# Attention with pairs of heads tied to the tiles of v, remainders on VectorE, x on one queue, and conv's output parts ahead of the next tile

## The chip, the cores and the metric

The kernel runs on one core of a Trainium2 chip. The metric is the device time of one execution in microseconds, as the median of three runs. Engines are TensorE (PE, with its weight loads as PEld), VectorE (DVE), ScalarE (ACT), GpSimd (POOL) and SyncE (SP), which here only issues DMAs. L12 is line 12 of the kernel before.

## The reference

A decoder trunk of two layers over 256 tokens of width 1024, all in float32. Each layer is a mixer followed by a PEER expert retrieval; each part has an RMS norm in front and a residual add behind.

```python
for i in range(DEPTH):                       # DEPTH = 2
    hn = rms_norm(x, norm_mix[i])
    if i % 2 == 0:                           # b, c, z = split(hn @ w_in); u = c * z
        x = x + short_conv_mixer(hn, ...)    # (b * causal_conv3(u)) @ w_out
    else:
        x = x + moba_mixer(hn, w_qkv, w_o)   # 16 heads of 64, rotary q and k, causal softmax
    x = x + peer_ffn(rms_norm(x, norm_ffn[i]), ...)
return rms_norm(x, norm_final)
```

With 256 tokens there is one block of keys, so the attention is plain causal attention: softmax(q k' / 8) v for each head, then the product with w_o.

## The kernel before

**Weight tiles.** All weights come in tiles ("items") of 128 x 1024 float32, 512 KB each, in one fixed list: 24 of the conv mixer's w_in (in the group order 1, 2, 0), 8 of its w_out, those of the first PEER, 24 of w_qkv (8 for q, 8 for k, 8 for v), 8 of w_o, those of the second PEER. A product in float32 is made of three cheaper ones: the weight is split into a rounded part hi and a remainder lo = raw - hi, the activations likewise into xh and xl, and TensorE sums hi·xh, hi·xl and lo·xh. One tile of such a product is twelve matmuls with 512 columns (L474, or L481 to L483 where two tiles are run together as a group, bank by bank; conv's w_in has 256 columns, L461).

**Splitting and loading.** `split_to` makes hi on ACT (L166) and lo on VectorE or, for the items in the set `on_pool`, on POOL (L171). raw, hi and lo have three buffers each, used in turn, so the split of tile n waits until TensorE has done with tile n-3, and the load of tile n (issued on SP's queue, L140 to L148) waits until the split of tile n-3 has read its buffer. `next_item` emits the split of the coming tiles (`prefetch`), then the matmuls of its tile, and then as many steps of side work as a budget in a queue (`add`, `run_side`) allows; `drain_side` empties that queue. `next_group` does the same for several tiles at once. The order in which the code emits is the order of each engine's instructions.

**Start.** x comes in four loads, on SP's and ACT's queues in turn, the norm's gain first on ACT's. TensorE runs 14 dummy matmuls (`warm`, L291), spreads the gain over the partitions (L269), runs 8 more, and then turns the normed x (L365), whose parts ACT and VectorE copy (L370, L375).

**Conv mixer.** After the third group of w_in, VectorE multiplies the gate into the result, four parts of it (L596), ACT casts each part to xh (L597), and VectorE takes the remainder xl (L591). Then w_out's eight tiles run. The first prefetch of w_out is emitted with the last tile of w_in, that is ahead of these parts.

**Attention.** While k's tiles run, q is rotated (`rope`, VectorE, L210, in four pieces by half of the tokens and of the heads), turned on TensorE (L654) and copied by ACT (L660). While v's tiles run, the side queue does the same with k (L654, L663), then the scores of the pairs of heads (L670 to L673, two banks for a pair), the row maxima on VectorE (`soft`, L677 to L681) and the exponentials on ACT (L684, L686): two pairs behind a tile. After v's last tile, v is copied out of PSUM, two parts on ACT (L729) and two on VectorE (L727), and the reciprocals are taken (L731). Then, for each pair of heads, `ptr` turns the weights on TensorE (L736, L738) into two of the four banks `hi4`, ACT copies one bank (L740) and VectorE the other (L741), and two pairs later `pv` multiplies them with v (L749 to L751). At the end the result is turned (L763), split (L766, L767), and w_o's tiles follow.

Of the kernel before, what the change touches and what calls it, by code (L numbers as in the profile page):

```python
# [22 lines left out]
D = 1024  # L23
# [9 lines left out]
WARM = 14  # L33
# [4 lines left out]
def trunk_kernel(ctx: ExitStack, tc, x, norm_mix, norm_ffn, conv_w_in, conv_w, conv_w_out,  # L38
# [79 lines left out]
    on_pool, on_dve, halved = set(range(3)), set(), {0}  # L118
    state = {"dma": 0, "tr": 0, "split": 0, "use": 0}
# [40 lines left out]
    def split_to(n):  # L160
        while state["split"] <= min(n, NI - 1):
# [4 lines left out]
            act.activation(HI[m % 3], src, AF.Copy)  # L166
# [49 lines left out]
    def next_item(mm, budget=0.0):  # L216

        n = state["use"]
        split_to(n)
        prefetch(n)  # L220
        mm(HI[n % 3], LO[n % 3])
        state.pop("rest", lambda: None)()
        state["use"] += 1
        run_side(budget)
# [28 lines left out]
    def load_x(eng, i, h):  # L253
        c = slice(h * 512, h * 512 + 512)
        eng.dma_start(x_in[:, i * D + h * 512:i * D + h * 512 + 512], x[0, i * 128:(i + 1) * 128, c])
# [16 lines left out]
    act.dma_start(GN[0:1], norm_mix[0:1])  # L272
    for i in range(2):
        load_x(sp, i, 0)
        load_x(act, i, 1)
# [19 lines left out]
    warm(8)  # L295
# [260 lines left out]
    def conv_mixer():  # L556
# [28 lines left out]
        for b in range(8):  # L585
            next_item(mm_wstat(lo4, b), 2.4)
# [13 lines left out]
        out_lo(3)  # L600
        rows_out(hi4, lo4[1::2], True)
# [5 lines left out]
    def attn_mixer():  # L607
# [80 lines left out]

        for a in range(2):
            pool.memset(qT[64 - 64 * a:128 - 64 * a, :, a], 0.0)  # L690
        for g, banks in ((0, lo4), (1, hi4), (2, lo4)):
            n = state["use"] - 3 * (g == 0)
            on_pool.update(k for k in range(n + 6, n + 14) if k % 3)
            if g:
                next_group(qkv_first(banks), None, 4.5)
            for b in range(2 if g else 3, 8):
                next_item(mm_tok(banks, XH[:, b], XL[:, b], False, b == 7), 9.0 if g == 2 else 2.5)
# [462 lines left out]
```

## Time and profile before

| | us |
|---|---|
| median of 3 runs (1857.15 to 1862.35) | 1858.34 |
| profiled execution | 1857.25 |
| its span in the trace | 1855.5 |
| TensorE busy | 1828.7 (99%) |
| VectorE busy | 1325.8 (71%) |
| ACT busy | 866.5 (47%) |
| POOL busy | 827.6 (45%) |
| TensorE's share of the chain that ended last | 89% |

A row of a timeline gives the start, the length, the engine, the line and operation, the tiles written and read with their shapes, the count of instructions put together, and in brackets the idle time of the engine in front of it with what ended it. Since matmuls are pipelined, their lengths overlap: the distance between starts tells the pace. PEclk in the windows is the clock that TensorE was granted in the stretch, 1.00 being 2.4 GHz and 0.50 1.2 GHz.

### The profile page before, as it was taken

To read this page: it belongs to the slowest core of one execution; us is meant where nothing else is said; L and a number is where in the kernel's file an instruction comes from. 1 tells how busy PE (TensorE), PEld (TensorE's weight loads), DVE (VectorE), ACT (ScalarE), POOL (GpSimd) and SP (SyncE) were. 2 spreads that over 40 slices of the span, in tenths; PEclk is the share of its full clock that TensorE was granted. 3 is DMA by queue.
4 is the path that set the end of the run, shared out by engine and by line. 5 is a ranking of instruction groups with operands and counts; after the bars stand their busy time and mean duration, and the time that the engine had idled before them with its cause. 6 is when DMAs were issued, how large, how long until landed. Compare 5 with 4: busy or idle time off the path is not lost.

```text
span 1855.5 us, 34248 instructions
## 1 busy us (share of the span) xinstructions
PE 1828.7 (99%) x12993; PEld 1642.2 (89%) x12993; DVE 1325.8 (71%) x2093; ACT 866.5 (47%) x1050; POOL 827.6 (45%) x564
## 2 busy tenths in 40 slices
PE   9999999999999999999999999999999999999998
PEld 8979999999998888888778799999999988888886
DVE  4648888777778886555554467897777788875555
ACT  4455445444444444444454454545434444444544
POOL 1048899999920000000251378899999600000000
PEclk9999999999999999999997999999999999999999
DMA  7566656555555555666551475555555555556554
GB/s 205 162 194 186 177 160 180 169 171 165 166 164 172 178 173 181 228 193 193 162 171 47 136 205 164 179 167 170 166 170 165 157 182 171 171 179 230 193 193 136
DMA packets 204587, 321.26 MB, mean 173 GB/s; under 512 B 26221, under 2 KB 157317, under 8 KB 203910
## 3 DMA queue, kind: packets, MB, share of 16 engines
q1 hardware_dynamic: 201716, 311.80, 54.8%
q10 hardware_dynamic: 2706, 7.28, 1.1%
q8 instruction: 101, 1.65, 0.4%
q14 instruction: 64, 0.52, 0.1%
HBM read 315.83 MB, written 3.15 MB: 172 GB/s over the span
## 4 chain that ended last, share of the span: by engine, by line
PE 89%; DVE 3%; DMA 3%; ACT 2%; issue 1%; POOL 1%; SPq 0%; DVEq 0%; ACTq 0%; POOLq 0%
PE psum L474 39%; PE psum L839 12%; PE psum L843 12%; PE psum L840 12%; PE psum L1003 3%; PE psum L461 3%; PE psum L503 1%; POOL lo L171 1%; DVE big L210 1%; PE psum L867 1%; DVE tr L155 1%; DVE lo L171 1%; ACT hi L166 1%; DMA raw<-in_peer_u_dram 1%; PE psum L483 1%
## 5 line engine op out<-in xcount | busy, mean ns | idle before, releaser
L171 POOL TENSOR_TENSOR lo<-tr,hi 128x512 fp32r<-128x512 f32 x496 | 732.5, 1516 | 47.2 <-ACT hi L166 43.6
L166 ACT ACTIVATE hi<-raw 128x1024 fp32r<-128x1024 f32 x336 | 355.5, 1061 | 458.1 <-PE psum L474 373.2
L171 DVE TENSOR_TENSOR lo<-raw,hi 128x1024 fp32r<-128x1024 f32 x301 | 372.4, 1238 | 272.0 <-ACT hi L166 263.8
L839 PE MATMUL psum<-xh,hi 128*128 128x256 f32 x2032 | 505.1, 286 | 1.0 <-ACT hi L166 1.0
L840 PE MATMUL psum<-xl,hi 128*128 128x256 f32 x2032 | 498.3, 283 | 0.0
L474 PE MATMUL psum<-hi,xh 128*128 128x512 f32 x1108 | 436.6, 396 | 1.3 <-ACT xh L597 1.3
L474 PE MATMUL psum<-hi,xl 128*128 128x512 f32 x1108 | 429.5, 389 | 0.0
L155 DVE STREAM_TRANSPOSE tr<-raw 128x1024 f32<-128x1024 f32 x256 | 317.3, 1239 | 143.1 <-POOL lo L171 113.4
L839 PEld LDWEIGHTS psum<-xh,hi 128*128 128x128 f32 x2032 | 389.3, 192 | 1.6 <-ACT hi L166 1.4
L840 PEld LDWEIGHTS psum<-xl,hi 128*128 128x128 f32 x2032 | 389.9, 192 | 0.2
L171 POOL TENSOR_TENSOR lo<-raw,hi 128x1024 fp32r<-128x1024 f32 (+1 forms) x42 | 85.8, 2059 | 593.2 <-ACT hi L166 494.2
L166 ACT ACTIVATE hi<-tr 128x1024 fp32r<-128x1024 f32 x256 | 270.0, 1057 | 123.6 <-DVE tr L155 87.0
L474 PE MATMUL psum<-lo,xh 128*128 128x512 f32 x1108 | 296.2, 389 | 0.0
L843 PE MATMUL psum<-xh,lo 128*128 128x256 f32 x2032 | 288.5, 284 | 6.3 <-POOL lo L171 6.3
L843 PEld LDWEIGHTS psum<-xh,lo 128*128 128x128 f32 x2032 | 263.1, 192 | 8.8 <-POOL lo L171 8.7
L474 PEld LDWEIGHTS psum<-lo,xh 128*128 128x128 f32 x1108 | 207.9, 188 | 43.5 <-DVE lo L171 0.2
L474 PEld LDWEIGHTS psum<-hi,xh 128*128 128x128 f32 x1108 | 208.0, 188 | 42.3 <-ACT xh L597 1.5
L474 PEld LDWEIGHTS psum<-hi,xl 128*128 128x128 f32 x1108 | 208.3, 188 | 41.0
L975 ACT ACTIVATE big<-psum 128x512 f32<-128x512 f32 x126 | 75.3, 597 | 285.7 <-PE psum L843 285.7
L1102 POOL TENSOR_TENSOR big<-xbuf,big 128x256 f32<-128x256 f32 x2 | 1.4, 733 | 379.7 <-DVE rstd L341 379.7
L988 DVE TENSOR_TENSOR xbuf<-iota_t,eT 128x1536 f16<-128x1536 f16 x128 | 126.7, 990 | 15.3 <-PE psum L1003 15.0
L996 DVE TENSOR_TENSOR xbuf<-xbuf,gT 128x1024 f16<-128x1024 f16 x128 | 99.6, 778 | 1.1
(172 smaller groups left out, 1473.3 us busy)
## 6 DMA issues: line engine op xcount, KB each, us to landing
raw<-in_peer_u_dram SPq DMA_DIRECT2D x1024, 128.0 KB, 2.8
raw<-in_peer_v_dram SPq DMA_DIRECT2D x256, 512.0 KB, 3.4
raw<-in_conv_w_in_dram SPq DMA_DIRECT2D x96, 128.0 KB, 2.6
raw<-in_attn_w_qkv_dram SPq DMA_DIRECT2D x96, 128.0 KB, 2.6
raw<-in_peer_w_q_dram SPq DMA_DIRECT2D x64, 128.0 KB, 2.6
raw<-in_conv_w_out_dram SPq DMA_DIRECT2D x8, 512.0 KB, 3.6
raw<-in_attn_w_o_dram SPq DMA_DIRECT2D x8, 512.0 KB, 3.3
x_dram<-xbuf ACTq DMA_DIRECT2D x2, 1024.0 KB, 4.8
```

What stands on the lines that cost most here:

```text
L155: dve.transpose(TR[m % 3].rearrange("p b (g i) -> p g b i", g=4), RAW[m % 3].rearrange("p (g m) -> p g m", m=256))
L166: act.activation(HI[m % 3], src, AF.Copy)
L171: eng.tensor_sub(LO[m % 3][:, c], src[:, c], HI[m % 3][:, c])
L461: pe.matmul(banks[c // 2][:, (c % 2) * 256:(c % 2) * 256 + 256], w[:, c * 128:c * 128 + 128], xx[:, b], start=(b == 0 and p == 0 and c % 2 ...
L474: pe.matmul(banks[j], x[:, j // 2 * 128:j // 2 * 128 + 128], w[:, j % 2 * 512:j % 2 * 512 + 512], start=(first and p == 0), stop=(last and ...
L839: pe.matmul(o, hi[:, s], XH[:, b], start=(b == 0), stop=False)
L840: pe.matmul(o, hi[:, s], XL[:, b], start=False, stop=False)
L843: pe.matmul(o, lo[:, s], XH[:, b], start=False, stop=(b == 7))
L975: act.activation(A[:, k - 1:k + 1].rearrange("p k t -> p (k t)"), bk, AF.Gelu)
L988: dve.tensor_tensor(HOT[s % 2].rearrange("p b (r k) t -> p b r k t", r=3), iota_t[:, None, None].to_broadcast([128, TOK // 2, 3, 64, 2]), ...
L996: dve.tensor_tensor(OHG[s % 2], one_hot[:, None].to_broadcast([128, 2, TOK // 2, 64, 2]), gT2[:, s, :, :, None, :].to_broadcast([128, 2, T ...
L1003: pe.matmul(o, pairs[:, t // 2, :, t % 2], OHG[s % 2][:, a, t // 2, :, t % 2], start=(a == 0), stop=(a == 1))
```

## The change

It has five parts.

1. Start: the 22 dummy matmuls run in one piece ahead of the spread of the gain. All four loads of x and the gain are issued on SP's queue, the gain third; ACT issues none of them.
2. Conv: the last tile of w_in's third group is emitted without its prefetch; that comes after the four parts of the result and their remainders.
3. Attention's splits: the remainders of w_qkv's and w_o's tiles that were on POOL are made on VectorE, all but one (tile 18 of the 32), and the hi casts of the tiles 21 to 25 too (L168 of the changed kernel).
4. k and the heads: the side queue is replaced by `run_heads(b)`, which ties each step to a tile of v. A pair's two banks are now every second one, by the pair's parity (`hi4[p % 2::2]`). Three of k's four ropes are emitted ahead of v's tiles, the fourth behind the turning of k's first half. Smaller budgets move each of the two turnings of q behind one tile more.
5. v and the weights: ACT copies v's first token half and VectorE its second. `ptr(0)` runs ahead of v's last tile.

```diff
-WARM = 14
+WARM = 22
...
-            act.activation(HI[m % 3], src, AF.Copy)
+            if m in hi_dve:
+                dve.tensor_copy(HI[m % 3], src)
+            else:
+                act.activation(HI[m % 3], src, AF.Copy)
...
-    def next_item(mm, budget=0.0):
+    def next_item(mm, budget=0.0, ahead=True):
...
-        prefetch(n)
+        if ahead:
+            prefetch(n)
...
-    act.dma_start(GN[0:1], norm_mix[0:1])
     for i in range(2):
-        load_x(sp, i, 0)
-        load_x(act, i, 1)
+        for h in range(2):
+            load_x(i, h)
+        if i == 0:
+            sp.dma_start(GN[0:1], norm_mix[0:1])
...
     warm(WARM)
     spread_gain(hi4[2:4])
-    warm(8)
...
         for b in range(8):
-            next_item(mm_wstat(lo4, b), 2.4)
+            next_item(mm_wstat(lo4, b), 2.4, b < 7)
         drain_side()
...
         out_lo(3)
+        prefetch(n - 1)
         rows_out(hi4, lo4[1::2], True)
...
+        def turn_k(h):
+            for c in range(2):
+                turn(kr, 4 * h + 2 * c, hi4[h + 2 * c])
+                put_k(4 * h + 2 * c, hi4[h + 2 * c])
+
+        def heads(*ps):
+            for f in (scores, soft):
+                for p in ps:
+                    f(p, hi4[p % 2::2])
...
+        def run_heads(b):
+
+            if b == 0:
+                turn_k(0)
+                rope(kr, hi4, 1, 1)
+                drain_side()
+            elif b == 2:
+                heads(0)
+                turn_k(1)
+            elif b < 6:
+                heads(2 * b - 5, 2 * b - 4)
+            elif b == 6:
+                heads(7)
+                ptr(0)
...
-            on_pool.update(k for k in range(n + 6, n + 14) if k % 3)
+            if g == 0:
+                on_pool.add(n + 18)
+                hi_dve.update(range(n + 21, n + 26))
             if g:
-                next_group(qkv_first(banks), None, 4.5)
+                next_group(qkv_first(banks), None, 2.5 * (g == 1))
+            if g == 2:
+                run_heads(0)
             for b in range(2 if g else 3, 8):
-                next_item(mm_tok(banks, XH[:, b], XL[:, b], False, b == 7), 9.0 if g == 2 else 2.5)
+                next_item(mm_tok(banks, XH[:, b], XL[:, b], False, b == 7), 2.5 * (g < 2))
+                if g == 2:
+                    run_heads(b)
...
-                for h in range(2):
-                    for i in range(2):
-                        rope(kr, hi4, i, h)
+                for i, h in ((0, 0), (1, 0), (0, 1)):
+                    rope(kr, hi4, i, h)
                 drain_side()
-                for h in range(2):
-                    pause(h)
-                    for c in range(2):
-                        add(0.1, turn, kr, 4 * h + 2 * c, hi4[h + 2 * c])
-                        add(0.1, put_k, 4 * h + 2 * c, hi4[h + 2 * c])
-                for p in range(0, 8, 2):
-                    pause()
-                    for f in (scores, soft):
-                        for a in range(2):
-                            add(0.5, f, p + a, hi4[2 * a:2 * a + 2])
-        for i in range(2):
-            for h in range(2):
-                v = va[:, i, h * 512:h * 512 + 512]
-                if h:
-                    dve.tensor_copy(v, lo4[2 * i + h])
-                else:
-                    act.activation(v, lo4[2 * i + h], AF.Copy)
+        for h in range(2):
+            act.activation(va[:, 0, h * 512:h * 512 + 512], lo4[h], AF.Copy)
+            dve.tensor_copy(va[:, 1, h * 512:h * 512 + 512], lo4[2 + h])
...
-            b0, b1 = hi4[2 * (p % 2):2 * (p % 2) + 2]
+            b0, b1 = hi4[p % 2::2]
...
         for p in range(10):
-            if p < 8:
+            if 0 < p < 8:
                 ptr(p)
```

In the lists below hi_72 to hi_74, lo_75 to lo_77 and raw_66 to raw_68 are the three buffers of each kind; line numbers of the changed kernel are a few higher (its L170 and L175 are L166 and L171, its L712 and L713 are L740 and L741).

VectorE around the end of v's tiles, before: the last minimum of a pair, a remainder, the copies of v, the reciprocals, and the copies of turned weights.

```order
L681 TENSOR_TENSOR big<-big 128x2
L171 TENSOR_TENSOR lo_75<-raw_66,hi_72 128x1024
L727 COPY big<-psum 128x512 x2
L731 RECIPROCAL big<-big 128x32
L741 COPY big<-psum 128x2x256 x6
```

The same place of the changed kernel:

```order
L687 TENSOR_TENSOR big<-big 128x2
L713 COPY big<-psum 128x2x256
L168 CAST hi_72<-raw_66 128x1024
L175 TENSOR_TENSOR lo_75<-raw_66,hi_72 128x1024
L761 COPY big<-psum 128x512 x2
L763 RECIPROCAL big<-big 128x32
L713 COPY big<-psum 128x2x256 x5
```

The first copy of turned weights has moved ahead of the split of a w_o tile, whose cast is now here too.

ACT from the turning of k to the first exponentials, before: two copies of turned k (L663) with a hi cast between and behind them.

```order
L663 ACTIVATE big<-psum 128x512 x2
L166 ACTIVATE hi_73<-raw_67 128x1024
L663 ACTIVATE big<-psum 128x512 x2
L166 ACTIVATE hi_74<-raw_68 128x1024
L684 ACTIVATE big<-psum,big 128x128
L686 ACTIVATE big<-psum,big 128x256
```

The same place of the changed kernel, where L669 copies k and L690 and L692 are the exponentials:

```order
L669 ACTIVATE big<-psum 128x512 x2
L170 ACTIVATE hi_73<-raw_67 128x1024
L690 ACTIVATE big<-psum,big 128x128
L692 ACTIVATE big<-psum,big 128x256
L690 ACTIVATE big<-psum,big 128x128
L692 ACTIVATE big<-psum,big 128x256
L669 ACTIVATE big<-psum 128x512 x2
```

The second half of k is copied behind the exponentials of the first pair of heads.

ACT at the end of w_in's third group in the conv mixer, before: casts of weights, and the four casts of the result (L597).

```order
L166 ACTIVATE hi_74<-raw_68 128x1024
L166 ACTIVATE hi_72<-raw_66 128x1024
L166 ACTIVATE hi_73<-raw_67 128x1024
L597 ACTIVATE xh<-psum 128x512 x4
```

The same place of the changed kernel (L602 casts the result):

```order
L170 ACTIVATE hi_74<-raw_68 128x1024
L170 ACTIVATE hi_72<-raw_66 128x1024
L602 ACTIVATE xh<-psum 128x512 x4
L170 ACTIVATE hi_73<-raw_67 128x1024
```

The hi cast of w_out's second tile has moved behind the four casts.

## Rows read from the trace of the kernel before

**Rows 1.** Windows: stretch, length, busy PE PEld DVE ACT POOL, PEclk, DMA, GB/s

```profile
929.50:932.90 3.40, 1.73 (x7) 0.84 (x6) 0.78 (x1) 1.49 (x2) 2.95 (x2) 1.00 0.53 154
971.30:977.40 6.10, 6.10 (x35) 4.97 (x33) 3.27 (x7) 4.01 (x17) 0.00 (x0) 1.00 0.42 127
992.40:999.20 6.80, 3.01 (x18) 1.85 (x17) 4.10 (x8) 4.50 (x15) 0.00 (x0) 0.98 0.45 142
999.00:1003.00 4.00, 4.00 (x22) 4.00 (x20) 0.92 (x2) 0.38 (x1) 0.00 (x0) 0.50 0.10 40
...
1029.70:1034.00 4.30, 4.30 (x20) 3.56 (x19) 0.95 (x2) 3.54 (x5) 1.49 (x1) 1.00 0.02 4
```

**Rows 2.** Timeline of PE, end of attention and the tiles of w_o

```profile
992.44 0.27 PE L736 MATMUL psum<-ident,big 128*128 128x128 f32 x1
...
998.69 0.47 PE L738 MATMUL psum<-ident,big 128*128 128x128 f32 x2 [1.69 <-DVE big L741]
...
1029.11 1.43 PE L474 MATMUL psum<-hi,xh 128*128 128x512 f32 x4
...
1045.58 0.50 PE L483 MATMUL psum<-lo,xh 128*128 128x512 f32 x1 [0.52 <-DVE lo L171]
```

**Rows 3.** Timelines of ACT and DVE, the same stretch

```profile
994.29 1.09 ACT L166 ACTIVATE hi<-raw 128x1024 fp32r<-128x1024 f32 x1
995.23 1.11 ACT L729 ACTIVATE big<-psum 128x512 f32<-128x512 f32 x2
...
995.41 1.23 DVE L171 TENSOR_TENSOR lo<-raw,hi 128x1024 fp32r<-128x1024 f32 x1 [2.67 <-ACT hi L166]
...
998.01 1.22 DVE L741 COPY big<-psum 128x512 f32<-128x512 f32 x2
```

**Rows 4.** Page, costliest groups: POOL's remainders of plain weight tiles

```profile
L171 POOL TENSOR_TENSOR lo<-raw,hi 128x1024 fp32r<-128x1024 f32 (+1 forms) x42 | 85.8, 2059 | 593.2 <-ACT hi L166 494.2
```

**Rows 5.** Chain that ended last: start, length, a run of 68 tiles

```profile
710.40 185.06 PE psum L474 x816
```

**Rows 6.** Timelines of PE and DVE at k's first tiles

```profile
932.51 0.50 PE L483 MATMUL psum<-lo,xh 128*128 128x512 f32 x1 [1.36 <-POOL lo L171]
...
939.67 1.04 PE L654 MATMUL psum<-ident,big 128*128 128x128 f32 x8
940.47 0.47 PE L474 MATMUL psum<-hi,xh 128*128 128x512 f32 x1
...
933.46 1.34 DVE L210 TENSOR_TENSOR big<-psum,big 128x512 f32<-128x512 f32 x3
...
935.44 1.34 DVE L210 TENSOR_TENSOR big<-psum,big 128x512 f32<-128x512 f32 x3
```

**Rows 7.** Timelines of ACT and DVE, k's turning and the first heads

```profile
961.55 1.09 ACT L663 ACTIVATE big<-psum 128x512 f32<-128x512 f32 x2 [0.29 <-PE psum L654]
...
971.01 0.37 ACT L684 ACTIVATE big<-psum,big 128x128 f32<-128x128 f32 x1 [3.78 <-DVE big L680]
...
974.25 1.06 ACT L166 ACTIVATE hi<-raw 128x1024 fp32r<-128x1024 f32 x1
...
963.74 3.41 DVE L171 TENSOR_TENSOR lo<-raw,hi 128x1024 fp32r<-128x1024 f32 x1
969.50 1.21 DVE L677 TENSOR_REDUCE big<-psum 128x3 f32<-128x384 f32 x2 [2.35 <-PE psum L673]
```

**Rows 8.** Timelines of PE, DVE and ACT, the start of w_out in conv

```profile
86.34 1.19 PE L474 MATMUL psum<-hi,xh 128*128 128x512 f32 x4 [1.34 <-ACT xh L597]
...
86.32 0.69 DVE L591 TENSOR_TENSOR xl<-psum,xh 128x512 fp32r<-128x512 f32 x1 [2.03 <-ACT xh L597]
...
88.84 0.60 ACT L597 ACTIVATE xh<-psum 128x512 fp32r<-128x512 f32 x1 [0.60 <-DVE psum L596]
```

**Rows 9.** Timeline of PE, the start

```profile
8.20 1.89 PE L291 MATMUL psum<-ident 128*128 128x256 bf16 x8
...
13.81 1.22 PE L461 MATMUL psum<-xh,hi 128*128 128x256 f32 x8 [0.69 <-ACT xh L370]
```

More of the change, by code (lines that the diff above doesn't have):

```diff
@@ L118, in trunk_kernel @@
     on_pool, on_dve, halved = set(range(3)), set(), {0}
+    hi_dve = set()
     state = {"dma": 0, "tr": 0, "split": 0, "use": 0}
@@ L251, in trunk_kernel, with load_x @@
     lo4, hi4 = B[0:4], B[4:8]
-    def load_x(eng, i, h):
+    def load_x(i, h):
         c = slice(h * 512, h * 512 + 512)
-        eng.dma_start(x_in[:, i * D + h * 512:i * D + h * 512 + 512], x[0, i * 128:(i + 1) * 128, c])
+        sp.dma_start(x_in[:, i * D + h * 512:i * D + h * 512 + 512], x[0, i * 128:(i + 1) * 128, c])
     def load_gain(w, l):
@@ L687, in soft, with ptr @@
                                scale=0.125, accum_out=sm[:, 1, h:h + 1])
+        def turn_k(h):
[6 more added lines that the diff above has]
+                    f(p, hi4[p % 2::2])
+        def ptr(p):
+            b0, b1 = hi4[p % 2::2]
+            for a in range(2):
+                pe.transpose(b0[:, a * 128:a * 128 + 128], S[:, p, a, 0:128], ident)
+                for j in range(2):
+                    pe.transpose(b1[:, a * 256 + j * 128:a * 256 + j * 128 + 128],
+                                 S[:, p, a, 128 + 128 * j:256 + 128 * j], ident)
+            act.activation(PT[p % 3][:, :, 0:128], b0[:, 0:256].rearrange("p (a s) -> p a s", a=2), AF.Copy)
+            dve.tensor_copy(PT[p % 3][:, :, 128:384], b1.rearrange("p (a s) -> p a s", a=2))
+        def run_heads(b):
[11 more added lines that the diff above has]
+                ptr(0)
         for a in range(2):
@@ L708, in attn_mixer @@
                 drain_side()
-                for h in range(2):
-                    for i in range(2):
-                        rope(kr, hi4, i, h)
+                for i, h in ((0, 0), (1, 0), (0, 1)):
+                    rope(kr, hi4, i, h)
                 drain_side()
-                for h in range(2):
-                    pause(h)
-                    for c in range(2):
-                        add(0.1, turn, kr, 4 * h + 2 * c, hi4[h + 2 * c])
-                        add(0.1, put_k, 4 * h + 2 * c, hi4[h + 2 * c])
-                for p in range(0, 8, 2):
-                    pause()
-                    for f in (scores, soft):
-                        for a in range(2):
-                            add(0.5, f, p + a, hi4[2 * a:2 * a + 2])
-        for i in range(2):
-            for h in range(2):
-                v = va[:, i, h * 512:h * 512 + 512]
-                if h:
-                    dve.tensor_copy(v, lo4[2 * i + h])
-                else:
-                    act.activation(v, lo4[2 * i + h], AF.Copy)
+        for h in range(2):
+            act.activation(va[:, 0, h * 512:h * 512 + 512], lo4[h], AF.Copy)
+            dve.tensor_copy(va[:, 1, h * 512:h * 512 + 512], lo4[2 + h])
         drain_side()
         dve.reciprocal(sm, sm)
-        def ptr(p):
-            b0, b1 = hi4[2 * (p % 2):2 * (p % 2) + 2]
-            for a in range(2):
-                pe.transpose(b0[:, a * 128:a * 128 + 128], S[:, p, a, 0:128], ident)
-                for j in range(2):
-                    pe.transpose(b1[:, a * 256 + j * 128:a * 256 + j * 128 + 128],
-                                 S[:, p, a, 128 + 128 * j:256 + 128 * j], ident)
-            act.activation(PT[p % 3][:, :, 0:128], b0[:, 0:256].rearrange("p (a s) -> p a s", a=2), AF.Copy)
-            dve.tensor_copy(PT[p % 3][:, :, 128:384], b1.rearrange("p (a s) -> p a s", a=2))
         def pv(p):
```

## The prediction

> **What bounds the kernel now.** The first view is the granted clock and the busy time of each engine, stretch by stretch [rows 1]; the second is the timeline of TensorE over the end of attention [rows 2]. TensorE is busy nearly all of the span (table above), so there are only two ways to shorten it: fewer of its few microseconds of waiting, or a faster clock where it has work. The windows show that the second is there to be had. During the last tiles of v the clock is full (2.4 GHz) and TensorE has no idle time at all (6.10 of 6.10 us). From 992.40 to 999.20 it is busy 3.01 of 6.80 us. Right after, the clock stands at 0.50 (1.2 GHz) while TensorE works without a break, and at 1029.70 it is at 1.00 again. So some 30 us of work run at half speed, and what stands ahead of the fall is the one stretch in which TensorE mostly waits.
>
> Why it waits there is read from the other two engines in the same microseconds [rows 2, 3]. The transposes of the attention weights (L736, L738) go into two pairs of banks; a pair comes free when ACT (L740) and VectorE (L741) have copied it. In front of those copies ACT still has a hi cast (1.09 us) and two copies of v (1.11 us), VectorE a remainder (1.23 us, itself held 2.67 us by that hi cast) and two copies of v; its first two copies at L741 start at 998.01. TensorE's gap of 1.69 us names L741 as its releaser, and VectorE's remainder names the hi cast.
>
> **The change, part by part.** Sums are made against the profiled execution, 1857.25 us, of which the span is 1855.5; the median of the three runs is 1858.34, 1.1 us above it, which is no more than they scatter.
>
> *End of attention.* ptr(0) now stands before v's last tile, so its two copies run under that tile; the hi casts of the last v tiles are VectorE's and no longer ACT's; the copies of v are one pair on each engine as before. After the last tile ACT owes two copies of v and then L740's copies, nothing else. VectorE owes the cast and the remainder of a wo tile before its copies of v, but the buffer they need is free one tile earlier, so 2.72 us of matmuls (185.06 us for 816, twelve to a tile [rows 5]) cover them (1.23 and, as below, about as much). TensorE meets ptr(1) and ptr(2), 1.2 us at the 0.10 us of a transpose (eight from 939.67 to 940.47 [rows 6]), while v is copied in 1.11 us. I take 0.8 us of waiting for the whole stage, between 0 and 2. The price of the stage: from 992.44 to 1029.11 are 36.67 us now [rows 2]. The first 6.8 us hold 3.01 of work at the full clock; the other 29.9, at half, are 14.96 at full. 3.01 + 14.96 + 0.8 = 18.8, a gain of **17.9** if the clock stays up. With 2 us of waiting it is 16.7, with none 18.7.
>
> *Tiles of wo.* The first runs partly at half clock: 1.43 us for four matmuls, 1.19 for four at the full clock [rows 2, 8], so 0.2. At 1045.58 TensorE waits 0.52 for a VectorE remainder [rows 2] that now stands behind no slow POOL remainder of its row of tiles. **-0.7**, if the wait only shrinks to a third -0.4, if it stays -0.2.
>
> *Tiles of q and k.* At the group of the first two k tiles TensorE is busy 1.73 of 3.40 us [rows 1], 1.36 of the gap at a remainder on POOL [rows 6]; a remainder costs 2.06 us on POOL [rows 4] and 1.23 on VectorE [rows 3], and VectorE was idle. That is -1.7. The new wait: the first turning of q stands one tile later, after two more tiles (group end 936.95 - 1.7, plus 2 x 2.72, 940.7). VectorE has the remainder of tile 11 ahead of q's two ropes now. Its hi cast waits until the group is nearly through (about 934.6); 1.09 + 1.23 later, 936.9, the ropes start; one takes 1.98 (933.46 to 935.44 [rows 6]), two end at 940.9. With the transfer late by a microsecond it is 941.9. A wait of 0.2 to 1.2, I take 0.5. **-1.2**, between -1.5 and -0.5.
>
> *Tiles of v with the heads.* Here the change adds: VectorE gets every remainder but one, and casts. Now a round of tile and two pairs of heads takes 6.1 us, all TensorE's, with VectorE busy 3.27 [rows 1]. A remainder and a cast come to it. No row shows a VectorE cast of 128x1024 from SBUF; it is bounded by ACT's 1.09 below and by twice a remainder above, and I take the remainder's 1.23, the same shape read and written. 3.27 + 1.23 + 1.23 = 5.7 is under 6.1, so the rounds hold; at 2.5 for the cast they would be 0.9 too long. Three waits are new. (1) The group of v's first two tiles meets remainders that stand between ropes on VectorE: 0 to 1.23, I take 0.5. (2) The first turning of k stands behind three ropes instead of two: 0 to 0.6, I take 0.3. (3) scores(1) needs the banks that turn_k(1) used, and these come free by put_k(1), which ACT has behind the exponentials of pair 0. From scores(0) the chain is row maxima up to the first exponential, 1.51 us (969.50 to 971.01 [rows 7]), one pair's exponentials, 1.62 (half of 971.01 to 974.25), and put_k, 1.09 [rows 7]: 4.22. TensorE fills it with eight transposes and a tile, 0.80 + 2.72 = 3.52. So it waits 0.7, and if VectorE is still at the remainder ahead of the maxima, 1.9. I take 1.2. Together **+2.0**, from 0.7 to 3.7.
>
> *Conv.* The wait of 1.34 us ahead of w_out's first tile [rows 8] goes: ACT's four casts no longer stand behind the hi cast of the second tile. That cast is late now instead. VectorE's 2.03 us of waiting [rows 8] go with it, so the fourth cast ends near 88.84 + 0.60 - 2.0 = 87.4, hi at 88.5; w_out's second tile wants it at 85.0 + 2.72 = 87.7. It waits 0.8, then about 0.3 for the remainder, which stays on POOL at 2.06. The buffer comes free about 2 us later and with it the transfers behind it, on SP's queue: 0 to 2.0 of it may arrive at the last tiles, I take 0.8. **+0.6**, between -0.2 and +1.8.
>
> *Start.* The same 22 warm-up matmuls, x on one queue with no issue on ACT. The first weights matmul now waits 0.69 us [rows 9]; earlier loads can take that at most. TensorE works in order, and warm-ups that filled a wait for x now run before the spread of the gain, so up to 1.9 (eight of them [rows 9]) may come back. **-0.4**, between -0.7 and +1.9.
>
> Sum: -17.9 - 0.7 - 1.2 + 2.0 + 0.6 - 0.4 = -17.6, so 1857.25 - 17.6 = **1839.6**. Bounds of the terms all at one end give 1836.1 and 1847.2.
>
> **Rivals.** *The clock falls all the same.* The stage after the last tile is made of transposes and of narrow matmuls, and no row shows that such work keeps a high clock up: from 999 on TensorE did nothing else, without a gap, and the clock stayed at half until the matmuls of wo. For it speaks that just this; against it, that the mean clock of 992.40 to 999.20, with eighteen of these instructions in it, is still 0.98 [rows 1]: it fell only after the 3.8 us of idle time. Then 14.96 us come back: 1839.6 + 15.0 = 1854.6. Falling halfway gives about 1847. The Trainium skill, in "TensorE: Matmul & The Clock Gate", section "Part 4: PE-mode transpose", says that transposes on TensorE do not count as busy for the clock in the way that matmuls do; the trace agrees in that the clock came back only at wo, but there the stage had other matmuls too. By that rule this rival is what happens.
>
> *VectorE becomes the bound in the rounds of heads.* Remainders have run at 3.41 us instead of 1.23 in this very stage [rows 7]. If this holds for two or three more of them, the five rounds are longer by up to 1 us each: 1844.6.
>
> *The new wait lowers the clock earlier (slower).* scores(1) waits for put_k(1), behind maxima and exponentials. If that wait and those at turn_k close by reach the idle share of 992.40 to 999.20 (3.8 of 6.8 us), the clock falls there, in the first rounds. It decides between that and the 1.67 of 3.40 us at 929.50, at full clock through [rows 1]. The price is 30 us at half clock, 15.0, and 2.6 of waiting beyond the 1.2; if the end of attention also falls, again 15.0: 1839.6 + 32.6 = 1872.2. A remainder slowed to 3.41 us ahead of the maxima is what would bring it; against it, that POOL, whose remainders run beside it now, has only one left.
>
> *The change doesn't do what it says.* The order of the instructions shows that it does: on VectorE one cast and one remainder are left ahead of v's copies, on ACT nothing. If it did not, the time would be 1857.
>
> **How the numbers follow.** Forecast 0.74; clock falls all the same 0.15; VectorE the bound 0.07; falls earlier 0.04. A difference under 0.3% (5.6 us) can't be told from no change. The forecast and the VectorE case are both faster by over 0.3%: 0.81, and of the second rival's halfway fall 0.01, so 0.82 in all; the full fall, 1854.6, is within 0.3%: 0.14; slower 0.04. The range reaches from 1834 (the terms' low end and a microsecond of scatter) to 1850, past the VectorE case and a halfway fall; the full fall and the slower case lie outside, a little under 2 in 10.
>
> **What would show it.** Right: in the changed profile the granted clock is 1.00 in the stage of L749's counterpart, pairs of 1.9 us (six transposes, twelve narrow matmuls) instead of about 3.7, TensorE's gap after the last v tile under 1 us; no wait for POOL at k's first group; at scores(1) a gap of 0.7 to 1.9 with ACT's put_k as releaser; a gap near 0.8 ahead of w_out's second tile. Wrong: a clock of 0.50 after v's last tile with TensorE busy (first rival), VectorE without gaps through the rounds and TensorE waiting for remainders (second), the clock at half from the first rounds on (third).

## The result, and the profile after

| | us |
|---|---|
| before, median of 4 runs (1857.15 to 1862.35) | 1859.05 |
| changed, median of 4 runs (1836.84 to 1838.54) | 1837.53 |
| ratio, with its 95% interval | 0.9883 (0.9866 to 0.9900) |
| profiled execution of the changed kernel, and its span | 1837.48, 1835.4 |

The change takes 21.5 us off the median. The forecast of 1839.6 us, against 1837.5 measured, took 17.6 off the profiled execution of 1857.25; between the two profiled executions the change is 19.8. The two traces can be laid side by side at the starts of the same TensorE instructions. "Stage" is what happened between a row and the one above it.

| TensorE starts | before | after | stage measured | stage forecast |
|---|---|---|---|---|
| first matmul with weights | 13.81 | 11.89 | -1.9 | -0.4 |
| transposes of the norm behind the conv mixer | 107.96 | 107.23 | +1.2 | +0.6 |
| k's first group (all of the first PEER before it) | 929.26 | 928.38 | -0.2 | 0 |
| v's first group | 955.09 | 953.25 | -1.0 | -1.2 |
| end of v's last tile (after: 993.54, less 0.57 for the early ptr(0)) | 992.44 | 992.97 | +2.4 | +2.0 |
| first tile of w_o | 1029.11 | 1010.47 | -19.2 | -17.9 |
| transposes of the norm behind w_o | 1051.76 | 1032.08 | -1.0 | -0.7 |
| end of the span | 1855.5 | 1835.4 | -0.4 | 0 |

The windows of the changed kernel (stretch, length, busy time of PE, PEld, DVE, ACT and POOL with counts, granted clock, DMA share, GB/s) answer to [rows 1]:

```profile
959.00:965.00 6.00, 5.44 (x31) 4.19 (x30) 5.90 (x12) 2.95 (x4) 0.00 (x0) 1.00 0.34 99
965.00:971.00 6.00, 5.17 (x30) 4.10 (x29) 4.78 (x8) 2.69 (x10) 0.00 (x0) 1.00 0.50 156
971.00:977.00 6.00, 6.00 (x34) 4.91 (x34) 4.77 (x10) 3.33 (x16) 0.00 (x0) 1.00 0.23 84
...
994.00:1001.00 7.00, 7.00 (x68) 7.00 (x66) 3.86 (x8) 1.96 (x6) 0.00 (x0) 1.00 0.23 77
1001.00:1008.50 7.50, 7.50 (x71) 7.50 (x71) 3.28 (x6) 2.58 (x6) 0.00 (x0) 1.00 0.11 35
```

Read the last two rows first: in the stage of transposes and narrow matmuls TensorE is busy 7.00 of 7.00 and 7.50 of 7.50 us, and the clock is 1.00, where it was 0.50 from 999.00 on. The 7.50 us hold 71 instructions; before, 4.00 us held 22, so 9.5 a microsecond against 5.5. In the first two rows the new price stands: TensorE idles 0.56 and 0.83 us there, with VectorE busy 5.90 of 6.00 us in the first of them. From 971 on TensorE has no idle time in a round of heads, with VectorE busy 4.77 of 6.00.

TensorE's timeline at the end of v, and VectorE's next to it, answer to [rows 2, 3]:

```profile
990.15 0.27 PE L708 MATMUL psum<-ident,big 128*128 128x128 f32 x1
...
993.54 0.27 PE L708 MATMUL psum<-ident,big 128*128 128x128 f32 x1
...
994.86 0.33 PE L771 MATMUL psum<-big 128*128 128x64 f32 x2
...
1008.56 2.15 PE L785 MATMUL psum<-ident,big 128*128 128x128 f32 x16
1010.47 0.71 PE L479 MATMUL psum<-hi,xh 128*128 128x512 f32 x2
```

```profile
991.83 0.69 DVE L168 CAST hi<-raw 128x1024 fp32r<-128x1024 f32 x1
992.55 1.23 DVE L175 TENSOR_TENSOR lo<-raw,hi 128x1024 fp32r<-128x1024 f32 x1
993.70 1.28 DVE L761 COPY big<-psum 128x512 f32<-128x512 f32 x2
...
995.15 1.22 DVE L713 COPY big<-psum 128x512 f32<-128x512 f32 x2
```

There is no bracket on any of TensorE's rows: not one wait from the early ptr(0) at 990.15 to the first tile of w_o. VectorE's cast and remainder run under v's last tile (990.72 to 993.54) and end some 0.2 us behind it; the copies of v follow at once.

### The profile page after: what moved, and what is told of

It is laid out like the page before. It is cut to its first block, busy times and chain, and to the rows that moved or that the text cites. A ratio compares the mean times of both kernels' runs of the same rounds, so it can differ in the third digit from the quotient of the medians.

```text
span 1835.4 us, 34236 instructions
## 1 busy us (share of the span) xinstructions
PE 1811.3 (99%) x12993; PEld 1626.6 (89%) x12993; DVE 1339.4 (73%) x2113; ACT 861.6 (47%) x1045; POOL 790.5 (43%) x549
## 4 chain that ended last, share of the span: by engine, by line
PE 88%; DVE 5%; DMA 3%; ACT 2%; issue 1%; POOL 1%; SPq 1%; DVEq 0%; ACTq 0%; POOLq 0%
PE psum L479 39%; PE psum L861 12%; PE psum L865 12%; PE psum L862 12%; PE psum L1025 3%; PE psum L466 3%; DVE big L214 2%; PE psum L508 1%; DVE lo L175 1%; DVE tr L156 1%; POOL lo L175 1%; PE psum L889 1%; ACT hi L170 1%; DMA x_dram<-xbuf 1%; DMA raw<-in_attn_w_qkv_dram 0%
## 5 line engine op out<-in xcount | busy, mean ns | idle before, releaser
L175 POOL TENSOR_TENSOR lo<-tr,hi 128x512 fp32r<-128x512 f32 x496 | 732.2, 1513 | 47.1 <-ACT hi L170 44.5
L175 DVE TENSOR_TENSOR lo<-raw,hi 128x1024 fp32r<-128x1024 f32 x316 | 387.9, 1228 | 259.1 <-ACT hi L170 244.5
L170 ACT ACTIVATE hi<-raw 128x1024 fp32r<-128x1024 f32 x331 | 349.8, 1060 | 451.5 <-PE psum L479 383.8
L170 ACT ACTIVATE hi<-tr 128x1024 fp32r<-128x1024 f32 x256 | 270.1, 1057 | 122.1 <-DVE tr L156 79.8
L175 POOL TENSOR_TENSOR lo<-raw,hi 128x512 fp32r<-128x512 f32 (+1 forms) x27 | 49.0, 1835 | 610.3 <-ACT hi L170 600.6
```

Of the source, the lines that this page charges most:

```text
L175: eng.tensor_sub(LO[m % 3][:, c], src[:, c], HI[m % 3][:, c])
```

## Experiments: what lowers the clock

The theory behind the forecast: the clock fell because TensorE stood still, and what it does next only runs at the clock that it finds. The rival: transposes and matmuls of 64 columns don't keep the clock up. The changed kernel speaks for the first by itself, but it changes the waits and the order at once. Three kernels add nothing but a wait to it, or a wait and work to fill it.

**Two extra VectorE operations.** The only edit, k = 2:

```diff
         drain_side()
         dve.reciprocal(sm, sm)
+        for _ in range(2):
+            dve.tensor_sub(XL[:, 0:4], XH[:, 0:4], XH[:, 4:8])
```

> The changed kernel with two extra subtractions of 128x1024 on VectorE behind the copies of v (their result is overwritten before it is used). They hold up VectorE's copy of ptr(1)'s weights by 2.5 us, so that TensorE stands still about 1.9 us ahead of ptr(3), and is otherwise busy. If idle time has to be as long as in the kernel before (3.8 of 6.8 us) to lower the clock: it stays at 1.00 and the time is the wait alone, 1837.5 + 1.9 = 1839.4. Rival (in transposes and narrow matmuls any gap of 1 to 2 us lowers the clock): half clock from there on, about 12 us of work at half that stay after the gap, so 1839.4 + 12 = 1851.

TensorE's row where it waits:

```profile
997.10 0.44 PE L710 MATMUL psum<-ident,big 128*128 128x128 f32 x2 [1.81 <-DVE big L713]
```

Eight executions split in two: five took 1838.1 to 1840.8 us with a mean clock of 0.997 to 0.999, three 1850.1 to 1851.9 with 0.993. The profiled one is the fastest of the first kind, so the 1.81 us were measured where the clock stayed up; that the gap is as long in the other kind is assumed. The edit alone lowers the clock in some executions and not in others; where it does, the price is some 11 us between the medians of the two kinds, near the 12 worked out from the rest of the stage. So both theories had part of it: in this place the clock can fall without a gap of 3.8 us.

**Four extra operations**, the same edit with k = 4:

> The same with four extra subtractions: TensorE stands still about 4.3 us in one piece ahead of ptr(3), all else as in the changed kernel. My theory: the clock falls as in the kernel before, the rest of the stage (about 12 us at the full clock) runs at half, time 1837.5 + 4.3 + 12 = 1854 (1850 to 1857). Rival (idle time doesn't lower the clock; it was the kind of work that stood there, or the tile of v just ahead): clock 1.00, time 1841.8.

```profile
996.00:1002.70 6.70, 2.38 (x20) 2.19 (x19) 6.41 (x8) 0.38 (x1) 0.00 (x0) 0.79 0.23 77
1002.70:1010.00 7.30, 7.30 (x37) 7.30 (x36) 1.38 (x2) 0.77 (x2) 0.00 (x0) 0.50 0.01 2
```

These windows are the kernel before over again: a stretch with TensorE busy 2.38 of 6.70 us, then 0.50 with TensorE never idle. TensorE stands still for 4.33 us up to 1001.97, and two windows inside that gap show that the clock is down before any further work comes:

```profile
998.00:999.50 1.50, 0.00 (x0) 0.00 (x0) 1.47 (x2) 0.00 (x0) 0.00 (x0) 1.00 0.00 0
1000.00:1001.90 1.90, 0.00 (x0) 0.00 (x0) 1.86 (x4) 0.00 (x0) 0.00 (x0) 0.50 0.00 0
```

Ten executions, all between 1852.7 and 1856.6, median 1854.62; 1854 was expected.

**Four extra operations, and forty matmuls in the gap.**

```diff
         for p in range(10):
+            if p == 3:
+                for _ in range(40):
+                    pe.matmul(lo4[1][:, 0:256], i16[:, 0:128], i16, start=True, stop=True)
             if 0 < p < 8:
                 ptr(p)
```

> The kernel with four extra subtractions, and forty matmuls of 128x256 in bf16 on data nobody reads, on TensorE ahead of ptr(3), that is in the 4.3 us of waiting. VectorE's delay is unchanged, so TensorE's own work comes as late as in the kernel with four subtractions; only the idle time is gone. My theory: clock 1.00, time 1837.5 + 4.3 = 1841.8 (1841 to 1843), some 12 us below the kernel without the forty. Rival: as slow as that kernel, near 1854, or the clock falls in part.

```profile
996.00:1002.70 6.70, 6.70 (x62) 6.15 (x61) 5.11 (x7) 0.77 (x2) 0.00 (x0) 1.00 0.01 2
```

1840.12 us (1839.8 to 1842.2). VectorE does the same extra work as in the kernel of 1854.62, and TensorE more: the forty matmuls compute nothing. They buy 14.5 us, and the kernel's 1840.12 is a little below the 1841 to 1843 expected. TensorE's useful work is the same narrow work in both; only the idle time is gone.

**The kernel before, filled.** The counterpart on the other side: nothing of the change, and 24 idle-time matmuls in the stall.

```diff
         def ptr(p):
             b0, b1 = hi4[2 * (p % 2):2 * (p % 2) + 2]
+            if p == 2:
+                keep_busy(8)
             for a in range(2):
                 pe.transpose(b0[:, a * 128:a * 128 + 128], S[:, p, a, 0:128], ident)
+                if (p, a) == (2, 0):
+                    keep_busy(16)
```

> The kernel before, with nothing of the change, and 24 matmuls of 128x256 in bf16 on data nobody reads: eight ahead of the third pair's transposes, sixteen between the first and the second of these, which is where TensorE stood still 1.43 and 1.69 us. The copies that TensorE waits for come no earlier. My theory (idle time lowers the clock, the kind of work doesn't): idle time falls from 3.8 to about 1.5 us, the clock stays at 1.00, and the 15 us come back: 1842 to 1845. Rival (it was the narrow work, or the clock falls in part of the executions): 1850 to 1858.

TensorE's timeline there, and the window behind it:

```profile
996.74 0.44 PE L746 MATMUL psum<-ident,big 128*128 128x128 f32 x2 [0.17 <-ACT big L686]
...
998.35 0.44 PE L746 MATMUL psum<-ident,big 128*128 128x128 f32 x2 [0.48 <-ACT big L686]
...
999.78 1.03 PE L735 MATMUL psum<-ident 128*128 128x256 bf16 x8 [0.66 <-ACT big L729]
...
1000.76 1.91 PE L735 MATMUL psum<-ident 128*128 128x256 bf16 x16
```

```profile
1003.00:1011.00 8.00, 8.00 (x76) 8.00 (x75) 3.75 (x7) 1.54 (x5) 0.00 (x0) 1.00 0.04 16
```

1845.78 us, against 1858.73 for the kernel before next to it: ratio 0.9926 (0.9910 to 0.9943), a little above the 1842 to 1845 expected. The gaps are 0.17, 0.48 and 0.66 us now instead of 0.16, 0.48, 1.43 and 1.69, and 76 instructions run in 8.00 us. Some 13 of the change's 21.5 us can be had with matmuls on data that nobody reads; from v's first group to w_o's first tile the two traces differ by 14.3 (74.02 us before, 59.69 filled). That settles what lowers the clock: the stall, not the kind of work. The kind of work matters the other way round: once the clock was down, transposes and narrow matmuls without a gap, 26.10 us of them at 0.50 in the kernel with four extra operations, didn't bring it back; there as in the kernel before it came back only at w_o's first tile.

## Experiments: which part of the change takes the stall away

**ptr(0) back behind the last tile.**

```diff
             elif b == 6:
                 heads(7)
-                ptr(0)
...
-            if 0 < p < 8:
+            if p < 8:
                 ptr(p)
```

> The changed kernel with one step undone: ptr(0) stands behind v's last tile again, as before the change. My theory (the clock fell because TensorE stood still for more than half of some 7 us, and hi casts and remainders in front of the copies were the larger part of that): TensorE has ptr(0) and ptr(1), 1.2 us, while v is copied, then waits about 0.7 us for VectorE's copy behind two copies of v; clock 1.00 through the stage, time 1838 to 1839.5. Rival (the early ptr(0) is what holds the clock up): TensorE waits 2 us or more and the stage runs at half clock, time near 1853.

```profile
996.10 0.44 PE L710 MATMUL psum<-ident,big 128*128 128x128 f32 x2 [0.67 <-DVE big L713]
```

1839.42 us (1839.28 to 1839.51); the clock stays at 1.00. The wait is 0.67 us, where 0.7 was expected. The time is 1.9 us longer, but the early ptr(0) is worth only some 0.5 of it: from v's first group to w_o's first tile this kernel takes 57.73 us and the changed one 57.22, and its profiled execution is 1.4 late at k's first group already (929.75 against 928.38), which the start and conv bring, not this edit. The clock doesn't hang on ptr(0).

**The hi casts of the last tiles back on ACT** (the set `hi_dve` left empty).

> The changed kernel with the hi casts of the tiles 21 to 25 on ACT again. My theory (these casts are covered, since their buffers come free a tile ahead): ACT goes from 3.35 to 4.4 us busy in a round of 6, TensorE waits nowhere longer than 0.7 us, clock 1.00, time 1837 to 1838.5. Rival (ACT's hi casts in front of the copies were what held TensorE up before): a gap of 1 to 2 us at the transposes, in which the clock falls in some or all executions, 1839 to 1852.

This went against my expectation: ten executions, five at 1841.5 to 1843.8 us, five at 1853.0 to 1855.7 with mean clocks of 0.989 to 0.992. The profiled one is of the first kind. The rows of TensorE, ACT and VectorE show the chain:

```profile
994.20 0.37 ACT L690 ACTIVATE big<-psum,big 128x128 f32<-128x128 f32 x1 [2.49 <-DVE big L686]
...
996.06 1.08 ACT L170 ACTIVATE hi<-raw 128x1024 fp32r<-128x1024 f32 x1
```

```profile
991.74 1.23 DVE L175 TENSOR_TENSOR lo<-raw,hi 128x1024 fp32r<-128x1024 f32 x1 [2.87 <-ACT hi L170]
992.88 1.02 DVE L683 TENSOR_REDUCE big<-psum 128x3 f32<-128x384 f32 x2
...
997.17 1.23 DVE L175 TENSOR_TENSOR lo<-raw,hi 128x1024 fp32r<-128x1024 f32 x1 [2.27 <-ACT hi L170]
998.31 1.28 DVE L760 COPY big<-psum 128x512 f32<-128x512 f32 x2
```

```profile
995.17 0.33 PE L708 MATMUL psum<-ident,big 128*128 128x128 f32 x1 [0.85 <-ACT big L692]
995.97 0.44 PE L710 MATMUL psum<-ident,big 128*128 128x128 f32 x2 [0.48 <-ACT big L692]
...
997.68 0.43 PE L770 MATMUL psum<-big 128*128 128x64 f32 x2 [0.28 <-ACT big L759]
999.05 0.43 PE L771 MATMUL psum<-big 128*128 128x64 f32 x2 [0.94 <-DVE big L760]
```

The buffer was free early, as I had said; but on ACT the cast stands behind the exponentials of the pairs before, VectorE's remainder waits 2.87 and then 2.27 us for it, and VectorE's maxima and copies of v stand behind that remainder. Each engine waits for the other in turn. With the cast on VectorE, cast and remainder are one piece of VectorE's own. TensorE loses 2.55 us in four gaps between 994.3 and 999.1 in this execution, in which the clock stayed up; in half of the executions of this kernel it fell, and none of those was profiled. Of the three edits undone one at a time in this section, this one does most for the stall; the new split of v's copies and the order of the heads were not undone.

**Remainders on POOL again**, as the kernel before had them; all else changed.

```diff
+            on_pool.update(k for k in range(n + 6, n + 14) if k % 3)
             if g == 0:
-                on_pool.add(n + 18)
                 hi_dve.update(range(n + 21, n + 26))
```

> The changed kernel with the remainders on POOL for the tiles that had them there before the change (two of three from tile 7 of w_qkv on); all else as changed. My theory: the wait at k's first group comes back (1.7 to 2.2 us) and some of the one at w_o (0.5), the end of attention keeps its clock, time 1840 to 1841. Rival (POOL's remainders, late and slowing VectorE, were the cause of the stall): gaps of 2 us or more at the end of attention and half clock there, 1853 or more.

```profile
930.72 0.50 PE L488 MATMUL psum<-lo,xh 128*128 128x512 f32 x1 [1.34 <-POOL lo L175]
956.29 0.50 PE L488 MATMUL psum<-lo,xh 128*128 128x512 f32 x1 [1.66 <-POOL lo L175]
```

1838.46 us (1837.1 to 1839.3), 0.9 above the changed kernel, less than the 2.5 to 3.5 that I expected; the ranges of the two overlap, so the time alone doesn't tell them apart. By stages, moving fifteen remainders to VectorE is worth some 1.5 us: undone, the tiles of q and k take 0.6 us more, those of w_o up to the norm 1.1 more, the rest of attention 0.2 less. The waits for POOL are back, 1.34 and 1.66 us, and so is one of 0.53 at w_o, for VectorE; in exchange VectorE has room, and the waits that the changed kernel has at the turning of q, at the turning of k and ahead of scores(1) (1.06, 0.56, and 0.83 in two gaps, below) are gone but for 0.18. POOL's slow remainders are no cause of the stall.

## Experiments: the start, conv, and the new waits

**14 and 8 warm-ups again, x on one queue** (the constant back to 14, `warm(8)` back behind the spread).

> The changed kernel with 14 warm-up matmuls ahead of the spread of the gain and 8 behind it, as before the change; x stays on one queue. My theory (the unbroken run lets the clock rise before the spread, which then takes 2.0 instead of 3.7 us): the spread ends near 8.2, the eight run to 9.9, the first matmul with weights starts at 13.1 to 13.8 instead of 11.9: 1838.8 to 1839.4. Rival (the earlier loads of x alone give the gain): first weights matmul at 11.9 still, 1837.5.

**Two queues again, 22 warm-ups in one run** (the four loads of x and the gain issued as before).

> The changed kernel with x and the gain on ACT's and SP's queues as before the change; the 22 warm-ups stay in one run. My theory: both halves of this part are needed, the parts of x land at 6.5, 6.8 and 8.7 us again and the norm of the second token tile ends 1.5 us later, first weights matmul at 13.3 to 13.8: 1838.9 to 1839.4. Rival (the clock alone gives the gain): 11.9, 1837.5.

TensorE's start, first with the split warm-ups, then with two queues:

```profile
1.39 3.17 PE L297 MATMUL psum<-ident 128*128 128x256 bf16 x14 [1.39 <-DVE ident L289]
4.49 2.23 PE L274 MATMUL psum<-big 1*128 1x512 f32 x4
...
10.14 0.66 PE L371 MATMUL psum<-ident,big 128*128 128x128 f32 x4 [1.04 <-DVE big L366]
11.48 0.93 PE L467 MATMUL psum<-xh,hi 128*128 128x256 f32 x4 [0.69 <-ACT xh L376]
```

```profile
6.20 3.78 PE L274 MATMUL psum<-big 1*128 1x512 f32 x4
...
14.27 0.98 PE L465 MATMUL psum<-xh,hi 128*128 128x256 f32 x6 [0.69 <-ACT xh L374]
```

The split warm-ups start the weights at 11.48, no later than the changed kernel (11.89), though the first of them run slowly and w_out begins at 83.98, behind the changed kernel's 82.90: 1838.27 us (1837.1 to 1839.9). Two queues start them at 14.27: 1839.69 us (1838.4 to 1839.8). That looks like the loads alone. But the pace of the spread tells more: 2.23 us for four matmuls in the one, 3.78 in the other, and 1.98 in the changed kernel. And the kernel of the next experiment, with the changed kernel's start unaltered, happened to run its profiled execution like this:

```profile
6.20 3.78 PE L274 MATMUL psum<-big 1*128 1x512 f32 x4
...
14.27 0.98 PE L466 MATMUL psum<-xh,hi 128*128 128x256 f32 x6 [0.69 <-ACT xh L375]
```

Same code as after, same early loads, and the times of two queues to a hundredth. Of ten profiled executions with this start nine begin the weights at 11.7 to 12.8 and one at 14.27. So the start has two courses, told apart by the pace of the spread, near 2 us or near 3.8. I read the two clocks from that pace alone; the record of the granted clock says 1.00 in both (from 6.20 to 9.90 in the slow one). Where the spread is slow, TensorE's own queue of warm-ups and spread sets the time: the two profiles with 22 warm-ups ahead of it agree, on two queues and on one. The kernel before, filled, which is shown above, has the other combination, two queues and a fast spread:

```profile
4.30 1.98 PE L269 MATMUL psum<-big 1*128 1x512 f32 x4
...
9.36 1.12 PE L365 MATMUL psum<-ident,big 128*128 128x128 f32 x4 [2.10 <-DVE big L360]
```

There TensorE waits 2.10 us for VectorE's normed x, and the weights begin at 13.72. With the same order of warm-ups, a fast spread and one queue (the split warm-ups) the first turning comes at 7.57 and not at 9.36, and the weights at 11.48. So both look needed, the fast spread and the earlier loads, as my theory for two queues said; where one of them is missing the weights begin between 13.7 and 14.3. Each combination but one rests on one or two profiles. Whether the change makes the fast spread likelier stays open: it was fast in ten of eleven profiled executions with one queue, and in one of three with two.

Even with one start the executions differ: in the ten profiled ones w_out's first matmul comes between 82.74 and 85.28. Two kernels whose times differ by less than these 2.5 us are therefore compared by their stages here.

**Conv's prefetch two parts earlier.**

```diff
             if j:
                 out_lo(j - 1)
+            if j == 1:
+                prefetch(n - 1)
         out_lo(3)
-        prefetch(n - 1)
```

> The changed kernel with conv's prefetch emitted behind the second of the four output parts and not behind all of them. w_out's first two tiles need only the first part, the third part only its fifth tile, so the hi cast of the second tile fits into ACT's wait between the second and third cast. My theory (the late hi cast and the POOL remainder behind it cost 0.71 + 0.38 us in the changed kernel, and 0.53 more at the last tiles): from w_out's first matmul to the first transposes of the norm 24.3 us become 22.8 to 23.3, time 1836.0 to 1836.5. Rival (the cast pushes back casts three and four, and TensorE waits there): 24 us or more, 1837.5 or above.

In the changed kernel the three waits of the forecast are there:

```profile
86.52 0.50 PE L479 MATMUL psum<-hi,xh 128*128 128x512 f32 x1 [0.71 <-ACT hi L170]
...
89.01 1.20 PE L479 MATMUL psum<-lo,xh 128*128 128x512 f32 x4 [0.38 <-POOL lo L175]
...
101.06 0.50 PE L488 MATMUL psum<-lo,xh 128*128 128x512 f32 x1 [0.53 <-DVE lo L175]
```

With the edit none of them is left, and w_out's first matmul to the norm's transposes takes 85.28 to 106.80, 21.5 us, instead of 82.90 to 107.23, 24.3: 2.8 us, more than the 1.0 to 1.5 expected. The nine other profiled kernels with the changed kernel's conv take 23.5 to 23.8 there, so the edit is worth 2.0 us at least. The time is 1836.71 us (1836.4 to 1837.6), 0.8 less than the changed kernel, with ranges that overlap; the profiled execution of this kernel had the late start, and so lost 2.4 of it again. Conv's part of the change, as made, costs more than it gains (+1.2 in the table above, +0.4 to +0.7 with the nine others); with the prefetch behind the second part it gains.

**k's second turning ahead of the first maxima.**

```diff
             elif b == 2:
-                heads(0)
-                turn_k(1)
+                scores(0, hi4[0::2])
+                turn_k(1)
+                soft(0, hi4[0::2])
```

> The changed kernel with the second turning of k ahead of the maxima and exponentials of the first pair (scores(0), turn_k(1), soft(0)), so that ACT copies k before them. My theory: the wait of 0.66 + 0.17 us ahead of scores(1) goes, the first exponentials come 1.1 us later and nobody waits for them: 1836.7. Rival (a round of heads is full enough that the delay of the exponentials comes back at the next pairs, which take over their banks): the gap only moves, 1837.5.

In the changed kernel, then with the edit, TensorE at scores(1):

```profile
970.08 0.32 PE L676 MATMUL psum<-big 128*128 128x384 bf16 x1 [0.66 <-ACT big L669]
970.57 0.32 PE L676 MATMUL psum<-big 128*128 128x384 bf16 x1 [0.17 <-ACT big L669]
```

```profile
968.41 0.50 PE L676 MATMUL psum<-big 128*128 128x384 bf16 x2
```

The wait is gone and shows up nowhere later. The stage from v's first group to w_o's first tile falls from 57.22 to 55.66 us, more than the 0.8 expected, of which 0.4 is a shorter wait at the first turning of k. The time is 1836.77 us (1835.6 to 1837.8), as expected, though it alone, with ranges that overlap, wouldn't show it.

**Both, and one remainder on POOL** (tile 11 of w_qkv added to tile 18).

> Both edits together, and the remainder of tile 11 of w_qkv on POOL, so that q's ropes don't stand behind it on VectorE (TensorE waits 1.06 us for them at the first turning of q in the changed kernel). If all three hold: -1.3 - 0.8 - 1.0, 1834.4. If POOL's remainder is late for its own tile, the third gives nothing: 1835.4.

1833.74 us (1832.9 to 1833.9), ratio to the kernel before 0.9866 (0.9849 to 0.9882), 3.8 us under the changed kernel. The wait at q's first turning is 0.31 us instead of 1.06:

```profile
937.93 0.98 PE L661 MATMUL psum<-ident,big 128*128 128x128 f32 x7 [0.31 <-DVE big L214]
```

This is the best of all the kernels here.

## Why the prediction was right, and where it was not

Against 1857.25 the changed kernel's profiled execution is 19.8 us lower (20.1 in the span), where 17.6 stood. The two misses that matter are 1.5 us at the start and 1.3 at the end of attention, both to the good; the first is in part luck, as said below.

*The clock.* The main term rested on one reading: TensorE stood still 3.8 of 6.8 us, then half clock [rows 1]. The chance of 0.15 for a fall all the same belonged to work that wouldn't hold the clock up. It was right, and the wait added, filled, and filled in the kernel before shows why. The Trainium skill, in "TensorE: Matmul & The Clock Gate", section "Part 4: PE-mode transpose", says that transposes don't count as busy in the way that matmuls do. The traces agree with it in that the mixture of transposes and narrow matmuls didn't bring the clock back, and differ in that the same mixture, without a gap, kept it at 1.00 in the changed kernel; there the rows decide. A stretch of transposes alone was not run.

*End of attention*, -19.2 where -17.9 stood. The step that was too careful is the 0.8 us of waiting: there was none. The other 0.5 is in the work: 17.5 us in all, where the sum had 3.01 + 14.96. The cover that it named, cast and remainder under v's last tile, was closer than forecast: behind the copy of ptr(0)'s weights they began 1.1 us into that tile and ended some 0.2 us after it, yet VectorE was done with ptr(1)'s weights about 0.4 us before TensorE came back to their bank at 996.26. That is because the cast on VectorE took 0.69 us. The forecast had bounded it by ACT's 1.09 below, which is another engine's time and no bound, and by 2.5 above, and taken 1.23; at 1.23 the half microsecond more would, by my estimate, have used up what was to spare. The Trainium skill gives a reason in "VectorE: DVE Perf Modes", section "Mode 2×_2P — use both read ports for one tensor": a copy with one source, both ends in SBUF, may use both read ports even in float32, which an operation on two tensors can't. The 0.69 against 1.23 for the remainder agrees with that.

*Tiles of v with heads*, +2.4 for +2.0, and each of its three waits is in the trace: 0.54 at the remainder of the first group (0.5 forecast), 0.56 at the first turning of k (0.3), 0.66 and 0.17 ahead of scores(1), with ACT's put_k as releaser (0.7 to 1.9, 1.2 taken). VectorE is busy 4.7 to 4.8 of 6.00 us in the full rounds, so that rival fell.

```profile
940.61 0.98 PE L660 MATMUL psum<-ident,big 128*128 128x128 f32 x7 [1.06 <-DVE big L214]
955.08 0.50 PE L488 MATMUL psum<-lo,xh 128*128 128x512 f32 x1 [0.54 <-DVE lo L175]
960.40 0.98 PE L660 MATMUL psum<-ident,big 128*128 128x128 f32 x7 [0.56 <-DVE big L214]
```

*Tiles of q and k*, -1.0 for -1.2: the wait for POOL went, and the one at q's ropes is 1.06 us, inside its 0.2 to 1.2, at the far end: two remainders stand ahead of the second rope (VectorE's at 934.21 and 937.34), where the forecast had counted one.

*Conv*, +1.2 for +0.6: hi late by 0.71 (0.8 forecast), the remainder by 0.38 (0.3), the last tiles by 0.53 (0.8). The edit that removes them gave 2.8 us back, more than these 1.6. A gap is counted from the modelled end of matmuls that overlap; counted by the distance between starts above the usual 0.23, TensorE lost 0.87, 0.54, 0.23 and 0.70, some 2.3. The last of the three waits is 0 to 0.36 us in the nine other profiled kernels with this conv, whose stage is +0.4 to +0.7: the forecast's size, and the +1.2 is an execution at the far end.

*Start*, -1.9 for -0.4, outside its bounds of -0.7 to +1.9. The step that failed is "earlier loads can take that at most": the wait of 0.69 us [rows 9] is still there in every kernel, and all that lies ahead of it moved. The forecast took the spread at the pace of the trace before, 3.7 us; it took 1.98 in the changed kernel's trace, and the earlier loads then let the first turning follow at once. That the spread was fast is not shown to come from the change. With the slow one, as in the one execution of ten, the time would have been near 1839.9 (an estimate: 2.4 us more at w_out's first matmul), so the start's share of the miss is luck as far as the record goes.

*Wo*, -1.0 for -0.7: the wait of 0.52 went wholly.

## What to carry to other kernels

Where the granted clock is low while TensorE is busy, look at what it did just before: a few microseconds of waiting can cost many times their length (here 3.8 us of waiting, and then 30 us of work at half speed). Such a stall is worth removing at the other engines' queues (here a cast and its remainder on one engine, and copies that nothing long stands ahead of), and where it can't be removed, matmuls on data that nobody reads, in a free bank, take back most of the price: 13 of 21.5 us here. Moving work between engines trades one wait for another; ask of each moved instruction which in-order queue it now stands in, and ahead of whom.

## What was not expected of the hardware

The fall of the clock is not the same in every execution of one kernel. It fell in three of eight executions of the kernel whose profile has a gap of 1.81 us, in five of ten of the one with 2.55 us in four gaps, and in ten of ten of the one with 4.33 us; where it falls, one execution is some 11 us longer than the next. Such a kernel has two times, and a median over few runs shows either. In the kernel with 4.33 us the clock went down while TensorE was idle, and narrow work without a gap didn't bring it back. The start has two courses as well: the spread of the gain was fast in nine of ten profiled executions of one start, and w_out began between 82.74 and 85.28. And VectorE's cast of 128x1024 from SBUF, at 0.69 us, is faster than ACT's at 1.06 to 1.09.
